# A hand-run list scheduler gets a draft pass, new durations and a table of 262 priority shifts, and tiles are bound to the draft's buffers

## Chip, cores, metric

One core of one Trainium2 chip. The core has five engines with a queue each: TensorE (PE, matrix products), VectorE (DVE), ScalarE (ACT), GpSimd (POOL) and SyncE (SP), which here only issues DMAs. Each engine works through its own queue in order; across engines they synchronise by semaphores. The metric is the device time of one execution in microseconds; lower is better.

## What is computed

A two-layer decoder trunk on 256 tokens of width 2048, all in float32. Each layer is a token mixer and a SwiGLU, each wrapped in an adaLN modulation, a residual and a LayerNorm:

```python
for layer in range(DEPTH):
    shift, scale, gate = _ada(c, ada_w[layer, 0], ada_b[layer, 0])
    h = x * (1.0 + scale) + shift
    y = _mixer_ab(h, ...) if layer % 2 == 0 else _mixer_cd(h, positions, ...)
    x = _layer_norm(ALPHA * x + (1.0 + gate) * y, ln_g[layer, 0], ln_b[layer, 0])
    shift, scale, gate = _ada(c, ada_w[layer, 1], ada_b[layer, 1])
    y = _swiglu(x * (1.0 + scale) + shift, ffn_w_gate[layer], ffn_w_up[layer], ffn_w_down[layer])
    x = _layer_norm(ALPHA * x + (1.0 + gate) * y, ln_g[layer, 1], ln_b[layer, 1])
```

Mixer AB is one input projection, then eight mLSTM heads beside sixteen RWKV-7 heads, then one output projection. Mixer CD is the same with eight retention heads and eight gated-DeltaNet heads. `_ada` is a product of a vector with a 2048 by 6144 matrix. The weights are read once: 677 MB move in one execution.

## The kernel before

**Products.** Every weight is split into a high and a low half (`split`, lines 693 to 715): a 1 MB block is loaded into a `raw` tile by an SP DMA (line 690), ACT copies it to `hi` (line 713), DVE subtracts to get `lo` (line 714). `part` (line 718) then issues three TensorE products for each piece, hi by hi, hi by lo and lo by hi (lines 728 to 730), each with 512 columns in most blocks. One 1 MB block gives 24 such products. They are called the dense products below.

**adaLN.** The vector-matrix products don't use TensorE: `ada_unit` (line 635) loads 1 MB of `ada_w` and DVE multiplies and sums it (line 649). There are 192 such units, 32 of them before the first `h` is whole, the rest spread between the products by `fill`.

**Stages.** In the program's order: `first_products` (the first adaLN units and the first two blocks of columns), `mixer_ab` with `mix_out`, `ffn(0)`, `mixer_cd` with `mix_out`, `ffn(1)`. The mixers hold many small products, transposes and DVE and ACT steps that hang on one another: the triangular inverses (`inverses`, lines 1037 to 1090), the RWKV and mLSTM heads, the DeltaNet chain, and `norm` at the end of each sub-layer. The SwiGLU stages are nearly all dense products.

**Buffers.** Tiles come from pools with tags: `raw` has 3 buffers, `hi` and `lo` 3 each, the 8 KB tag `a` 5, `y` 3, `q4` 4, `tiny` 12; PSUM banks come in three tags (`g` 3, `m` 3, `c` 2). A tile can begin only when a buffer of its tag is free.

**The order.** The kernel doesn't leave the order of each engine's queue to the framework. After the whole program is written out, `Plan` (lines 208 to 526) reads the instruction list, works out the dependencies (`depend`), gives each instruction a duration (`cost`, `matmul`, `prepare`) and runs a list scheduler over a model of the five engines and one DMA pipe (`run`): at each moment an engine takes the ready instruction with the lowest priority number. The model holds a rate for the DMA pipe, a delay between engines, buffers per tag (as a count of free ones, opened in the order of first use), ACT table loads and a TensorE clock that falls to one half after a window of 3413 ns in which TensorE was little used. `impose` (line 522 on) then chains the instructions of each engine in the order found. Only the order is imposed; on the chip each instruction still waits for its semaphores, and which buffer of a tag a tile gets is chosen by the framework. The priorities are those of the program's order with the offsets of `high_priority`. The last lines of `body`:

```python
plan = Plan(tc, tc.nc, 250, k.after)
plan.prepare(0)
order, _ = plan.run([x.bass_priority for x in plan.ins])
plan.impose(order)
```

Of the kernel before, what the change touches and what calls it, by code (L numbers as in the profile page):

```python
# [12 lines left out]
F32 = mybir.dt.float32  # L13
# [190 lines left out]
WINDOW = 3413.0  # L204
SETS = {"Silu": 18, "Tanh": 18, "Sigmoid": 2, "Exp": 0, "Sin": 9}


class Plan:
# [3 lines left out]
    def __init__(self, tc, nc, soon=0.5, after={}):  # L212
        self.tc, self.nc, self.soon, self.rate = tc, nc, soon, 358.0
# [80 lines left out]
    def cost(self, i):  # L294

        x, e = self.ins[i], self.eng[i]
        sizes = []
        for o in list(x.ins) + list(x.outs):
            if hasattr(o, "bass_ap"):
                n = 1  # L300
                for s, c in o.ap[1:]:
                    n *= int(c)
                sizes.append(n)
        n = max(sizes or [1])
        op = x.opcode
        if e == "DVE":
            if op == "TensorScalarPtr":
                if x.is_scalar_tensor_tensor:
                    d = 2373 if len(x.outs) > 1 or n >= 2048 else 150 + n * 1.045 + (55 if n > 100 else 5)
                elif x.is_tensor_tensor_scan:  # L310
                    d = 200 + n * 2.1
                else:
                    ptr = sum(1 for o in list(x.ins)[1:] if hasattr(o, "bass_ap"))
                    d = 145 + n * (0.77 if ptr else 0.55) + (100 if ptr and n > 100 else 0)
            elif op == "TensorCopy":
                ps = any(o.bass_ap.tensor.name in self.psum for o in x.ins if hasattr(o, "bass_ap"))
                d = 150 + n * (1.045 if ps else 0.53)
            else:
                d = {"BNStats": 135 + n * 1.07, "BNStatsAggregate": 168, "StreamShuffle": 179 + n * 1.1, "Memset": 60 + n * 0.5,
                     "Reciprocal": 157 if n < 64 else 150 + 2 * n}.get(op, 150 + n * 1.045)  # L320
            return max(d - 60, 15), d
        if e == "Activation":
            if len(x.outs) > 1:
                d = 500
            else:
                d = 200 + n * 0.83 + (80 if any(hasattr(o, "bass_ap") and k == 1 for o, k in zip(list(x.ins)[1:], sizes[1:])) else 0)
                d = d if n > 64 else max(300, d)
            return max(d - 60, 15), d
        if e == "Pool":
            d = {"TensorScalarAffineSelect": 1130 if n > 300 else 520, "TensorTensor": 1300, "TensorScalarPtr": 1000, "Memset": 100 + n}.get(op, 100)  # L330
            return d, d
        return 50, 50

    def matmul(self, i):

        x = self.ins[i]
        n = int(np.prod([int(c) for s, c in x.outs[0].ap[1:]]))
        w, m = x.ins[0], x.ins[1]
        if "float32r" in str(w.dtype):
            return n / 2.4, 13.5  # L340
        if x.is_transpose:
            return 106.0, 3.0
        k = int(np.prod([int(c) for s, c in m.ap[1:]]))
        return 2 * n / 1.2, 2 * (max(k, n) / 1.2 + 4.5) - 2 * n / 1.2
# [4 lines left out]
    def run(self, priority, clock=True, log=None):  # L349
# [14 lines left out]
        free = {t[0]: t[1] for t in tag.values()}  # L364
# [20 lines left out]
        clk = [1.0, 0, 0.0]  # L385
        for i in range(N):
            if not left[i]:
                heapq.heappush(future[eng[i]], (0.0, priority[i], i))
# [14 lines left out]
        while left_n:  # L403
# [5 lines left out]
            while releases and releases[0][0] <= now:  # L409
                _, t = heapq.heappop(releases)  # L410
                free[t] += 1
                for i in gated.pop(t, ()):
                    heapq.heappush(avail[eng[i]], (priority[i], i))
            again = True
            while again:
                again = False
                for e in E:
# [4 lines left out]
                    while at[e] <= now and a:  # L422
# [6 lines left out]
                        if e == "PE":  # L429
                            st, over = self.pe[i]  # L430
# [14 lines left out]
                        for n in of.get(i, ()):  # L445
                            if n in opened:
                                continue
                            opened.add(n)
                            t = tag[n][0]
                            free[t] -= 1  # L450
                            head[t] += 1
                            for k in gated.pop(t, ()):
                                heapq.heappush(avail[eng[k]], (priority[k], k))
                        start[i] = now
                        if e == "PE":
                            z, rest = now, st
                            while rest > 1e-6:
# [10 lines left out]
                                clk[2] += step  # L468
# [4 lines left out]
                            done[i] = at[e] + 160 / clk[0]  # L473
                        elif i in self.bytes:
                            at[e] = now + 60
                            by = self.bytes[i]
                            dma = max(now + 500, dma) + by / self.rate
                            done[i] = max(dma + 1300, now + 2000)
                        else:
                            x = 0.0  # L480
                            if e == "Activation":
                                s = self.table(i)
                                if s is not None and s != tab:
                                    tab, x = s, 1283.0
                            at[e] = now + x + c
                            done[i] = now + x + d
# [4 lines left out]
                        for n in of.get(i, ()):  # L491
                            remaining[n] -= 1
                            ends[n] = max(ends[n], done[i])
                            if not remaining[n]:
                                heapq.heappush(releases, (ends[n] + 40, tag[n][0]))
                                heapq.heappush(events, (ends[n] + 40, 0))
                        for j in users[i]:
                            left[j] -= 1
                            r = at[e] if e == "PE" and eng[j] == "PE" else done[i] + 40
# [9 lines left out]
    def prepare(self, soon_pe=0.0):  # L509
        self.soon_pe = soon_pe  # L510
        self.costs, self.pe, self.bytes = {}, {}, {}
        for i, x in enumerate(self.ins):
            if self.eng[i] == "PE":
                self.pe[i] = self.matmul(i)
            elif x.opcode == "DMACopy":
                self.costs[i] = 60, 60
            else:
                self.costs[i] = self.cost(i)
# [10 lines left out]
class Trunk:  # L529
    def __init__(self, tc, ins, out, stack):  # L530
        self.tc, self.nc, self.ins, self.out = tc, tc.nc, ins, out
# [21 lines left out]

    def bank(self, kind="m"):

        return {"g": self.ps_g, "c": self.ps_c, "m": self.ps_m}[kind].tile([P, 512], F32, tag=kind, name=self.name(kind))

    def a8(self, shape, dt=F32):
        return self.a_p.tile(shape, dt, tag="a", name=self.name("a"))

    def y8(self, shape):
        return self.y_p.tile(shape, F32, tag="y", name=self.name("y"))

    def q4(self, shape, dt=F32):
        return self.mix.tile(shape, dt, tag="q4", bufs=4, name=self.name("q"))

    def t2(self, shape):
        return self.mix.tile(shape, F32, tag="t2", bufs=3, name=self.name("t"))

    def t1(self, shape):  # L570
        return self.mix.tile(shape, F32, tag="t1", bufs=3, name=self.name("s"))

    def f1(self, shape):
        return self.mix.tile(shape, F32, tag="f1", bufs=3, name=self.name("f"))

    def own(self, shape, tag, bufs, dt=F32):
        return self.mix.tile(shape, dt, tag=tag, bufs=bufs, name=self.name(tag))

    def tiny(self, shape, tag="tiny", bufs=12):
        return self.mix.tile(shape, F32, tag=tag, bufs=bufs, name=self.name("v"))  # L580
# [107 lines left out]
    def raw(self, src, room=None):  # L688
        w = room([P, 2048]) if room else self.raw_p.tile([P, 2048], F32, tag="raw", name=self.name("raw"))
# [3 lines left out]
    def split(self, src, n, ahead=2000, homes="ss", room=None):  # L693
# [3 lines left out]
        with self.tc.high_priority(offset=ahead):  # L697
            w = self.raw(src, room)
            parts = []
            for i, home in enumerate(homes):  # L700
                if home == "s":
                    hi = self.split_p.tile([P, 1024], F32R, tag="hi", name=self.name("hi"))
                    lo = self.split_p.tile([P, 1024], F32R, tag="lo", name=self.name("lo"))
# [188 lines left out]
    def norm(self, y, banks, stats, sub):  # L892
# [3 lines left out]
        acts = [self.h_p.tile([P, 2, 4, T], F32R, tag="h", name=self.name("h")) for _ in range(KG)]  # L896
# [435 lines left out]
    def first_products(self):  # L1332
# [7 lines left out]
        for g in range(KG):  # L1340
            h.append(self.h_p.tile([P, 2, 4, T], F32R, tag="h", name=self.name("h")))
# [553 lines left out]
def body(tc, ins, out):  # L1895
    with ExitStack() as stack:
        k = Trunk(tc, ins, out, stack)
# [18 lines left out]
OUT = "y_out"  # L1916

# [14 lines left out]
```

## Time and profile before

| | us |
|---|---|
| median of 3 runs | 2728.81 |
| fastest, slowest of the 3 | 2728.55, 2734.14 |
| the profiled execution's own time | 2744.2 |
| its span, first to last instruction | 2742.5 |
| TensorE busy in it | 2631.8 (96%) |
| VectorE busy in it | 2002.3 (73%) |
| ScalarE busy in it | 1272.7 (46%) |
| mean granted TensorE clock | 0.977 |

A busy share says that an engine had an instruction in work; for TensorE the end of an instruction is modelled, so a string of products with short stalls between them still shows as busy. The granted clock is the share of full speed that the throttle gave TensorE. The span is cut below into the kernel's stages: start (0 to 137 us), mixer AB with its output projection (137 to 754), first SwiGLU (754 to 1439), mixer CD (1439 to 2056), second SwiGLU (2056 to 2673), and the end.

### The profile page before, as it was taken

To read this page: it belongs to the slowest core of one execution; us is meant where nothing else is said; L and a number is where in the kernel's file an instruction comes from. 1 tells how busy PE (TensorE), PEld (TensorE's weight loads), DVE (VectorE), ACT (ScalarE), POOL (GpSimd) and SP (SyncE) were. 2 spreads that over 40 slices of the span, in tenths; PEclk is the share of its full clock that TensorE was granted. 3 is DMA by queue.
4 is the path that set the end of the run, shared out by engine and by line. 5 is a ranking of instruction groups with operands and counts; after the bars stand their busy time and mean duration, and the time that the engine had idled before them with its cause. 6 is when DMAs were issued, how large, how long until landed. Compare 5 with 4: busy or idle time off the path is not lost.

```text
span 2742.5 us, 33594 instructions
## 1 busy us (share of the span) xinstructions
PE 2631.8 (96%) x12906; PEld 2164.2 (79%) x12906; DVE 2002.3 (73%) x3153; ACT 1272.7 (46%) x1706; POOL 72.3 (3%) x88
## 2 busy tenths in 40 slices
PE   5699999999999999999999999999999999999997
PEld 3578777778788888888888888878878888888886
DVE  7897868878777777767777989776866665557457
ACT  2364445556644444434446554444454444443442
POOL 0000000110000000000000101000000000000000
PEclk8799989999999999999999999999999999999999
DMA  9967647555588788868856775675657675556554
GB/s 394 370 244 259 226 176 282 183 187 190 205 311 309 305 323 311 315 234 302 309 201 223 270 274 224 234 259 200 244 200 275 249 289 203 196 200 227 187 186 167
DMA packets 105659, 681.60 MB, mean 249 GB/s; under 512 B 11861, under 2 KB 15129, under 8 KB 27417
## 3 DMA queue, kind: packets, MB, share of 16 engines
q1 hardware_dynamic: 104346, 677.36, 66.7%
q8 instruction: 101, 1.65, 0.2%
q10 hardware_dynamic: 1152, 2.10, 0.2%
q14 instruction: 60, 0.49, 0.1%
HBM read 668.89 MB, written 10.52 MB: 248 GB/s over the span
## 4 chain that ended last, share of the span: by engine, by line
PE 78%; DVE 10%; DMA 8%; ACT 2%; issue 2%; SPq 0%; POOL 0%; DVEq 0%; ACTq 0%
PE g L728 24%; PE g L729 23%; PE g L730 23%; DVE lo L714 2%; DMA raw<-ada 2%; DMA a<-ada 2%; DVE raw L649 2%; DMA raw<-w_ab 1%; ACT hi L713 1%; DMA za<-ada 1%; PE m L973 1%; DMA y<-w_ab 1%; PE m L1253 0%; PE m L1086 0%; PE m L1271 0%
## 5 line engine op out<-in xcount | busy, mean ns | idle before, releaser
L714 DVE TENSOR_TENSOR lo<-raw,hi 128x1024 fp32r<-128x1024 f32 (+2 forms) x802 | 971.5, 1214 | 580.6 <-ACT hi L713 577.1
L713 ACT ACTIVATE hi<-raw 128x1024 fp32r<-128x1024 f32 (+2 forms) x802 | 842.6, 1052 | 1111.4 <-PE g L730 1035.5
L728 PE MATMUL g<-hi,h 128*128 128x512 f32 (+2 forms) x2312 | 911.0, 394 | 41.2 <-ACT h L792 37.3
L729 PE MATMUL g<-lo,h 128*128 128x512 f32 (+2 forms) x2312 | 908.3, 393 | 2.1 <-DVE lo L714 2.1
L730 PE MATMUL g<-hi,h 128*128 128x512 f32 (+2 forms) x2312 | 907.1, 393 | 0.0
L728 PEld LDWEIGHTS g<-hi,h 128*128 128x128 f32 x2312 | 440.6, 191 | 132.8 <-ACT h L792 40.1
L729 PEld LDWEIGHTS g<-lo,h 128*128 128x128 f32 x2312 | 440.5, 191 | 92.5 <-issue 4.3
L730 PEld LDWEIGHTS g<-hi,h 128*128 128x128 f32 x2312 | 440.1, 190 | 88.2 <-issue 3.6
L729 PE MATMUL g<-lo,a 128*128 128x512 f32 x920 | 359.0, 390 | 1.6 <-DVE lo L714 1.6
L728 PE MATMUL g<-hi,a 128*128 128x512 f32 x920 | 359.3, 391 | 0.0
L730 PE MATMUL g<-hi,a 128*128 128x512 f32 x920 | 358.8, 390 | 0.0
L649 DVE SCALAR_TENSOR_TENSOR raw<-raw,silu_c 128x2048 f32<-128x2048 f32 x82 | 187.4, 2286 | 32.1 <-DMA raw<-ada 24.3
L729 PEld LDWEIGHTS g<-lo,a 128*128 128x128 f32 x920 | 172.8, 188 | 37.0 <-DVE lo L714 2.0
L730 PEld LDWEIGHTS g<-hi,a 128*128 128x128 f32 x920 | 172.8, 188 | 35.6
L728 PEld LDWEIGHTS g<-hi,a 128*128 128x128 f32 x920 | 172.7, 188 | 35.5
L649 DVE SCALAR_TENSOR_TENSOR za<-za,silu_c 128x2048 f32<-128x2048 f32 x56 | 127.9, 2284 | 4.5 <-DMA za<-ada 4.5
L649 DVE SCALAR_TENSOR_TENSOR zt<-zt,silu_c 128x2048 f32<-128x2048 f32 x38 | 86.8, 2285 | 2.6 <-DMA zt<-ada 2.4
L1437 DVE SCALAR_TENSOR_TENSOR f<-c,cols_sb,f 128x253 f32<-128x253 f32 (+2 forms) x120 | 55.8, 476 | 4.4 <-ACT f L1434 3.9
L1638 POOL TENSOR_SCALAR s<-cons_sb,log_alpha 128x128 f32<-128x128 f32 x16 | 13.4, 852 | 1008.5 <-DVE log_alpha L1582 871.6
L649 DVE SCALAR_TENSOR_TENSOR a<-a,silu_c 128x2048 f32<-128x2048 f32 x16 | 36.3, 2285 | 0.0
L911 ACT ACTIVATE t<-m,affine 128x128 f32<-128x128 f32 x96 | 34.9, 469 | 0.1
L1094 POOL TENSOR_SCALAR_AFFINE_SELECT a<-a 128x512 f32<-128x512 f32 (+1 forms) x20 | 22.4, 1127 | 332.4 <-ACT a L1255 300.0
(480 smaller groups left out, 2122.2 us busy)
## 6 DMA issues: line engine op xcount, KB each, us to landing
raw<-gu SPq DMA_DIRECT2D x176, 1024.0 KB, 4.8
raw<-dn SPq DMA_DIRECT2D x88, 1024.0 KB, 4.8
raw<-ada SPq DMA_DIRECT2D x82, 1024.0 KB, 6.1
raw<-w_cd SPq DMA_DIRECT2D x60, 1024.0 KB, 4.8
za<-ada SPq DMA_DIRECT2D x56, 1024.0 KB, 7.0
raw<-w_ab SPq DMA_DIRECT2D x48, 1024.0 KB, 4.9
zt<-ada SPq DMA_DIRECT2D x38, 1024.0 KB, 7.1
a<-ada SPq DMA_DIRECT2D x16, 1024.0 KB, 17.1
```

The source lines that it names most:

```text
L649: v.scalar_tensor_tensor(w[:], w[:], 1.0, self.sc[:], ALU.mult, ALU.mult, accum_out=m[:, i:i + 1])
L713: nc.scalar.activation(hi[:, :2 * n], ws, AF.Copy)
L714: nc.vector.tensor_tensor(lo[:, :2 * n], ws, hi[:, :2 * n], ALU.subtract)
L728: mm(o, ah, wh, start=start and k == 0, stop=False)
L729: mm(o, ah, wl, start=False, stop=False)
L730: mm(o, al, wh, start=False, stop=stop and k == 3)
L911: nc.scalar.activation(h32[:, j, :], b[:, P * j:P * j + P], AF.Identity, bias=self.ab[:, sub + 1, 16 + k:17 + k], scale=self.ab[:, sub + 1 ...
L973: nc.tensor.transpose(b[:, P * k:P * k + P], gs[:, t, P * k:P * k + P], self.ident)
L1094: self.nc.gpsimd.affine_select(x, x, pattern=[[0, n] for n in dims] + [[1, P]], compare_op=ALU.is_gt if strict else ALU.is_ge, fill=0.0, b ...
L1437: v.scalar_tensor_tensor(o[:, d:T], b[:, T * j:T * j + T - d], self.col(wname, 4 * (tile0 + i + j) + 3 - d), o[:, d:T], ALU.mult, ALU.add)
L1638: nc.gpsimd.tensor_scalar(L[:], sl, self.gl[:, t, 4 * g + j:4 * g + j + 1], None, ALU.mult)
```

## The change

No instruction of the computation is added or removed. What changes is the order within each engine's queue and the buffer each tile uses.

1. **Two builds.** `kernel` builds the program twice. The first build runs `Plan.run` and raises `Drafted` with the order of each engine and the buffer that the model gave each tile. The second build writes the same program out again and imposes that order.
2. **Buffers.** In the second build each tile that goes through the new `Trunk.get` asks for a tag of its own buffer (`a.3`, say) with one buffer, the one that the draft gave it. The model now keeps a list of free buffers of each tag instead of a count and takes the one that was freed first.
3. **Durations.** `cost`, `matmul` and `prepare` get new constants, among them factors by engine (`MARGINS`), a DMA rate of 396 instead of 358, a DMA landing time and a delay between engines of 67 instead of 40 ns. The clock model counts small products at a part of their time, and a change of the shape of the products costs 92 ns.
4. **Priorities.** A table `PLACES` of 262 pairs adds a shift to the priority of each instruction from the given index on, up to the next pair.

```diff
+MARGINS = {'Activation': 0.9875423830141832, 'DVE': 1.0101153058187327, 'PE': 1.014122181386299, 'Pool': 1.1973257770806474}
+LAND, CROSS, RATE, SOON = 2471.8499431610267, 67.12701229691764, 396.01772112428813, 250.0
+PLACES = (
+    (0, 240), (16, 0), (18, 920), (21, 0), (31, 920), (32, 40), (58, 0), (212, -1920), (216, 0), (225, -1680), (277, -1920), (281, 0), (303, -1000),
+    (325, -8960), (340, -9280), (347, -8120), (373, 120), (380, -1080), (397, -7480), (406, 0), (476, -80), (531, -840), (560, 0), (568, -200),
...
+    (15285, 48.0463), (16983, 160), (17012, 0), (17182, -1720), (17198, 0), (17201, -360), (17208, -420),
+)
...
-                    d = 2373 if len(x.outs) > 1 or n >= 2048 else 150 + n * 1.045 + (55 if n > 100 else 5)
+                    d = 2285 if len(x.outs) > 1 or n >= 2048 else 150 + n * 1.045 + (55 if ptr and n > 30 else 0)
...
-            return max(d - 60, 15), d
+            return max(d - 82, 15), d
         if e == "Activation":
-            if len(x.outs) > 1:
-                d = 500
-            else:
-                d = 200 + n * 0.83 + (80 if any(hasattr(o, "bass_ap") and k == 1 for o, k in zip(list(x.ins)[1:], sizes[1:])) else 0)
-                d = d if n > 64 else max(300, d)
-            return max(d - 60, 15), d
+            d = 310 if len(x.outs) > 1 else 163 + n * 0.848 + (0 if ps else 35) + (0, 97, 190)[ptr]
+            return max(d - 100, 15), d
...
-        return 2 * n / 1.2, 2 * (max(k, n) / 1.2 + 4.5) - 2 * n / 1.2
+        r = int(m.ap[0][1])
+        if max(r, k, n) <= 32:
+            return 30.0, 10.0, 1
+        return 2 * n / 1.2, 2 * (max(k, n) / 1.2 + 4.8) - 2 * n / 1.2, (0 if r > 64 else 2 if r > 32 else 3)
...
-        free = {t[0]: t[1] for t in tag.values()}
+        free = {t[0]: list(range(t[1])) for t in tag.values()}
+        self.held = held = {}
...
-                            free[t] -= 1
+                            held[n] = free[t].pop(0)
...
+                            if form != shape:
+                                shape, over = form, over + 92
...
-                                clk[2] += step
+                                clk[2] += step * (1.0, 0.25, 0.5, 0.25)[form]
...
-                            dma = max(now + 500, dma) + by / self.rate
-                            done[i] = max(dma + 1300, now + 2000)
+                            dma = max(now + self.iss, dma) + by / self.rate
+                            done[i] = dma + self.land
...
+    def get(self, pool, shape, dt, tag, bufs, name):
+
+        name = self.name(name)
+        if name in self.slots:
+            tag, bufs = f"{tag}.{self.slots[name]}", 1
+        return pool.tile(shape, dt, tag=tag, bufs=bufs, name=name)
+
...
-        plan = Plan(tc, tc.nc, 250, k.after)
-        plan.prepare(0)
-        order, _ = plan.run([x.bass_priority for x in plan.ins])
+        plan = Plan(tc, tc.nc, SOON, k.after)
+        if draft is None:
+            plan.prepare(0)
+            shift = np.zeros(len(plan.ins))
+            for i, s in PLACES:
+                shift[i:] = s
+            order, _ = plan.run([x.bass_priority + s for x, s in zip(plan.ins, shift)])
+            raise Drafted(order, {n.rsplit("_", 1)[0]: s for n, s in plan.held.items()})
         plan.impose(order)
```

More of the change, by code (lines that the diff above doesn't have):

```diff
@@ L212, in __init__ @@
     def __init__(self, tc, nc, soon=0.5, after={}):
-        self.tc, self.nc, self.soon, self.rate = tc, nc, soon, 358.0
+        self.tc, self.nc, self.soon, self.rate = tc, nc, soon, RATE
         self.ins = [x for x in nc.cur_bb.bb.instructions if x.opcode != "TilePoolBoundary"]
@@ L296, in cost @@
         x, e = self.ins[i], self.eng[i]
[L297 to L304, printed above, removed]
+        size = lambda o: int(np.prod([int(c) for s, c in o.ap[1:]]))
+        aps = [o for o in x.ins if hasattr(o, "bass_ap")]
+        outs = [o for o in x.outs if hasattr(o, "bass_ap")]
+        n = max([size(o) for o in aps + outs] or [1])
+        ptr = sum(1 for o in aps[1:] if size(o) == 1)
+        ps = any(o.bass_ap.tensor.name in self.psum for o in aps + outs)
         op = x.opcode
@@ L312, in cost @@
                 else:
-                    ptr = sum(1 for o in list(x.ins)[1:] if hasattr(o, "bass_ap"))
                     d = 145 + n * (0.77 if ptr else 0.55) + (100 if ptr and n > 100 else 0)
             elif op == "TensorCopy":
-                ps = any(o.bass_ap.tensor.name in self.psum for o in x.ins if hasattr(o, "bass_ap"))
                 d = 150 + n * (1.045 if ps else 0.53)
             else:
-                d = {"BNStats": 135 + n * 1.07, "BNStatsAggregate": 168, "StreamShuffle": 179 + n * 1.1, "Memset": 60 + n * 0.5,
-                     "Reciprocal": 157 if n < 64 else 150 + 2 * n}.get(op, 150 + n * 1.045)
-            return max(d - 60, 15), d
+                d = {"BNStats": 135 + n * 1.07, "BNStatsAggregate": 175, "StreamShuffle": 175 + n * 1.05, "Memset": 100 + n * 0.5,
+                     "Reciprocal": 150 + n * 6}.get(op, 150 + n * 1.045)
+            return max(d - 82, 15), d
         if e == "Activation":
-            if len(x.outs) > 1:
-                d = 500
-            else:
-                d = 200 + n * 0.83 + (80 if any(hasattr(o, "bass_ap") and k == 1 for o, k in zip(list(x.ins)[1:], sizes[1:])) else 0)
-                d = d if n > 64 else max(300, d)
-            return max(d - 60, 15), d
+            d = 310 if len(x.outs) > 1 else 163 + n * 0.848 + (0 if ps else 35) + (0, 97, 190)[ptr]
+            return max(d - 100, 15), d
         if e == "Pool":
-            d = {"TensorScalarAffineSelect": 1130 if n > 300 else 520, "TensorTensor": 1300, "TensorScalarPtr": 1000, "Memset": 100 + n}.get(op, 100)
+            d = {"TensorScalarAffineSelect": 1100 if n == 512 else 900, "TensorTensor": 950, "TensorScalarPtr": 1200, "Memset": 610}.get(op, 100)
             return d, d
@@ L385, in run @@
         clk = [1.0, 0, 0.0]
+        shape = 0
         for i in range(N):
@@ L409, in run @@
             while releases and releases[0][0] <= now:
-                _, t = heapq.heappop(releases)
-                free[t] += 1
+                _, t, n = heapq.heappop(releases)
+                free[t].append(held[n])
                 for i in gated.pop(t, ()):
@@ L429, in run @@
                         if e == "PE":
-                            st, over = self.pe[i]
+                            st, over, form = self.pe[i]
                             hold = self.soon_pe
@@ L472, in run @@
                             at[e] = z + over / clk[0]
-                            done[i] = at[e] + 160 / clk[0]
+                            done[i] = at[e] + self.pel / clk[0]
                         elif i in self.bytes:
@@ L498, in run @@
                             left[j] -= 1
-                            r = at[e] if e == "PE" and eng[j] == "PE" else done[i] + 40
+                            r = at[e] if e == "PE" and eng[j] == "PE" else done[i] + self.lat
                             if r > ready[j]:
@@ L510, in prepare @@
         self.soon_pe = soon_pe
+        self.iss, self.land, self.pel, self.lat = 1300.0, LAND, 160.0, CROSS
         self.costs, self.pe, self.bytes = {}, {}, {}
@@ L513, in prepare @@
             if self.eng[i] == "PE":
-                self.pe[i] = self.matmul(i)
+                st, over, form = self.matmul(i)
+                self.pe[i] = st * MARGINS["PE"], over, form
             elif x.opcode == "DMACopy":
@@ L517, in prepare @@
             else:
-                self.costs[i] = self.cost(i)
+                self.costs[i] = tuple(c * MARGINS[self.eng[i]] for c in self.cost(i)) if self.eng[i] in MARGINS else self.cost(i)
             if x.opcode == "DMACopy":
@@ L529, with __init__ @@
 class Trunk:
-    def __init__(self, tc, ins, out, stack):
-        self.tc, self.nc, self.ins, self.out = tc, tc.nc, ins, out
+    def __init__(self, tc, ins, out, stack, slots):
+        self.tc, self.nc, self.ins, self.out, self.slots = tc, tc.nc, ins, out, slots
         def pool(name, bufs, **kw):
@@ L688, in raw @@
     def raw(self, src, room=None):
-        w = room([P, 2048]) if room else self.raw_p.tile([P, 2048], F32, tag="raw", name=self.name("raw"))
+        w = room([P, 2048]) if room else self.get(self.raw_p, [P, 2048], F32, "raw", 3, "raw")
         self.load = self.nc.sync.dma_start(w[:, :src.shape[-1]], src).ins.name
@@ L701, in split @@
                 if home == "s":
-                    hi = self.split_p.tile([P, 1024], F32R, tag="hi", name=self.name("hi"))
-                    lo = self.split_p.tile([P, 1024], F32R, tag="lo", name=self.name("lo"))
+                    hi = self.get(self.split_p, [P, 1024], F32R, "hi", 3, "hi")
+                    lo = self.get(self.split_p, [P, 1024], F32R, "lo", 3, "lo")
                 elif home == "a":
@@ L895, in norm @@
         self.ada(max(0, 48 * sub + 80 - self.ada_next))
-        acts = [self.h_p.tile([P, 2, 4, T], F32R, tag="h", name=self.name("h")) for _ in range(KG)]
+        acts = [self.get(self.h_p, [P, 2, 4, T], F32R, "h", 4, "h") for _ in range(KG)]
         dst = self.dram.tile([T, D], F32, name=self.name("x"))
@@ L1340, in first_products @@
         for g in range(KG):
-            h.append(self.h_p.tile([P, 2, 4, T], F32R, tag="h", name=self.name("h")))
+            h.append(self.get(self.h_p, [P, 2, 4, T], F32R, "h", 4, "h"))
             xs = [self.first_x(g, i) for i in range(2)]
@@ L1892, in mix_out, with body @@
         return self.norm(y, banks, stats, sub)
-def body(tc, ins, out):
+class Drafted(Exception):
+    pass
+def body(tc, ins, out, draft=None):
+    order, slots = draft or (None, {})
     with ExitStack() as stack:
-        k = Trunk(tc, ins, out, stack)
+        k = Trunk(tc, ins, out, stack, slots)
         k.setup()
@@ L1909, in body, with build @@
         k.ffn(1, x, h)
-        plan = Plan(tc, tc.nc, 250, k.after)
-        plan.prepare(0)
-        order, _ = plan.run([x.bass_priority for x in plan.ins])
+        plan = Plan(tc, tc.nc, SOON, k.after)
[6 more added lines that the diff above has]
+            raise Drafted(order, {n.rsplit("_", 1)[0]: s for n, s in plan.held.items()})
         plan.impose(order)
 OUT = "y_out"
+def build(bacc, tile, arrays, draft):
+    nc = bacc.Bacc("TRN2", target_bir_lowering=False, num_devices=1, dynamic_dma_scratch_size=1024)
+    ins = {k: nc.dram_tensor(k, a.shape, mybir.dt.from_np(a.dtype), kind="ExternalInput").ap() for k, a in arrays.items()}
+    out = nc.dram_tensor(OUT, (T, D), F32, kind="ExternalOutput").ap()
+    with tile.TileContext(nc) as tc:
+        body(tc, ins, out, draft)
+    return nc
 def kernel(**inputs):
@@ L1924 @@
     arrays = lay_out(**{k: np.asarray(v) for k, v in inputs.items()})
-    nc = bacc.Bacc("TRN2", target_bir_lowering=False, num_devices=1, dynamic_dma_scratch_size=1024)
-    ins = {k: nc.dram_tensor(k, a.shape, mybir.dt.from_np(a.dtype), kind="ExternalInput").ap() for k, a in arrays.items()}
-    out = nc.dram_tensor(OUT, (T, D), F32, kind="ExternalOutput").ap()
-    with tile.TileContext(nc) as tc:
-        body(tc, ins, out)
+    try:
+        build(bacc, tile, arrays, None)
+    except Drafted as d:
+        draft = d.args
+    nc = build(bacc, tile, arrays, draft)
     r = run_bass_kernel_spmd(nc, [arrays], core_ids=[0])
```

24 lines of the change are left out of this document (12 added, 12 removed), and 22 rows, old and new, of the table PLACES.

## The prediction

> **What bounds the kernel now.** I read the page's busy times and its slices first, then a table of busy time by stage, then who waits for whom.
>
> ```profile
> PE 2631.8 (96%) x12906; PEld 2164.2 (79%) x12906; DVE 2002.3 (73%) x3153; ACT 1272.7 (46%) x1706; POOL 72.3 (3%) x88
> ...
> PEclk8799989999999999999999999999999999999999
> ...
> GB/s 394 370 244 259 226 176 282 183 187 190 205 311 309 305 323 311 315 234 302 309 201 223 270 274 224 234 259 200 244 200 275 249 289 203 196 200 227 187 186 167
> ...
> 0.00:137.00 137.00, 78.39 (x291) 61.15 (x292) 110.66 (x126) 45.14 (x63) 0.28 (x5) 0.81 0.95 382
> 137.00:754.00 617.00, 593.57 (x3364) 478.21 (x3363) 495.12 (x1145) 334.06 (x575) 35.71 (x47) 0.96 0.60 217
> 754.00:1439.00 685.00, 685.00 (x3065) 567.14 (x3064) 499.16 (x496) 293.48 (x302) 0.00 (x0) 1.00 0.77 292
> 1439.00:2056.00 617.00, 604.04 (x3194) 503.05 (x3194) 493.93 (x969) 318.38 (x479) 36.30 (x36) 0.99 0.64 236
> 2056.00:2673.00 617.00, 616.83 (x2760) 510.39 (x2759) 352.92 (x334) 263.35 (x273) 0.00 (x0) 1.00 0.62 224
> 2673.00:2742.00 69.00, 53.92 (x238) 44.28 (x236) 50.53 (x84) 18.25 (x18) 0.00 (x0) 0.91 0.45 168
> ```
>
> A stage row gives the stretch and its length, busy time with count of PE, PEld, DVE, ACT and POOL, then the granted clock, the DMA share and GB/s. TensorE is the bound, but not everywhere alike. In the two SwiGLU stages (685 and 617 us) it works without a break at full clock: in 1302 us no order can gain. What an order can reach lies elsewhere:
>
> - start: 137.0 - 78.4 = 58.6 us idle, beside a DMA share of 0.95;
> - mixer AB: 617.0 - 593.6 = 23.4 us idle, and 4% of the clock, 617 x 0.04 = 24.7 us;
> - mixer CD: 617.0 - 604.0 = 13.0 us idle, and 617 x 0.01 = 6.2 us;
> - end: 69.0 - 53.9 = 15.1 us.
>
> Since a busy PE can hide short stalls, I check AB by counting. Below are the first and the last of 28 dense products in a row from the timeline (start, length), the row of the tiles `g`, which nearly all dense products write, for AB, and a run of 16 small products from the chain.
>
> ```profile
> 799.81 0.39 PE L729 MATMUL g<-lo,h 128*128 128x512 f32 x1
> ...
> 805.93 0.39 PE L729 MATMUL g<-lo,h 128*128 128x512 f32 x1
> ...
> 137.00:754.00 617.00, 430.28 (x1693) 316.09 (x1694) 5.22 (x8) 20.00 (x34) 0.96 0.60 217
> ...
> 451.75 1.79 PE m L1037 x16
> ```
>
> 27 steps in 805.93 - 799.81 = 6.12 us are 0.227 us for one dense product; 1693 of them are 384 us. A small one takes 1.79 / 16 = 0.112 us; the other 3364 - 1693 = 1671 are then about 187 us. 617 - 384 - 187 = 46 us are left, against 23.4 + 24.7 = 48 us that idle time and clock show. The estimate is rough (wider forms cost more, packed ones less), but it finds the same loss, so I work with the visible one.
>
> Whom TensorE waits for in AB, then in CD, then in the start (waiter, releaser: us in total, times, longest):
>
> ```profile
> PE c L1201 <- DVE za L1104: 4.6, 2, 2.5
> PE m L908 <- ACT y L903: 1.9, 2, 1.4
> ...
> PE m L908 <- ACT y L903: 4.1, 4, 1.7
> PE m L1079 <- DVE a L1071: 1.7, 2, 1.5
> ...
> PE g L728 <- ACT h L792: 46.7, 7, 13.0
> ```
>
> In the mixers there is no single large wait, only many of one or two microseconds, each where an instruction at the head of TensorE's queue waits for a DVE or ACT step while dense products that could run stand behind it. That is what an order can mend.
>
> **The change, part by part.** *Instructions.* None is added or removed, so every engine's work stays; all that can change is who stands where.
>
> *Durations.* I compare the model's new constants with the trace.
>
> ```profile
> 113.17 2.28 DVE L649 SCALAR_TENSOR_TENSOR raw<-raw,silu_c 128x2048 f32<-128x2048 f32 x1
> 115.38 0.08 DVE L649 DVE_READ_ACCUMULATOR raw<-raw,silu_c 128x1 f32 x1
> 115.38 1.22 DVE L714 TENSOR_TENSOR zt<-y,zt 128x1024 fp32r<-128x1024 f32 x1
> ...
> L911 ACT ACTIVATE t<-m,affine 128x128 f32<-128x128 f32 x96 | 34.9, 469 | 0.1
> L903 ACT ACTIVATE y<-y,v,v 128x512 f32<-128x512 f32 x24 | 18.3, 811 | 10.8 <-DVE v L922 10.8
> ...
> raw<-gu SPq DMA_DIRECT2D x176, 1024.0 KB, 4.8
> ```
>
> An adaLN unit holds DVE for 115.38 - 113.17 = 2.21 us. The old model says 2373 - 60 = 2313 ns, the new one (2285 - 82) x 1.0101 = 2225 ns: the old one had 0.10 us too much in each of 192 units. For the ACT step of line 911 the old model gives 200 + 128 x 0.83 + 80 = 386 ns, the new one (163 + 128 x 0.848 + 190) x 0.9875 = 456 ns, against 469 measured; for line 903 it is 705 and 822 x 0.9875 = 812, against 811. So on DVE and ACT the draft lies much nearer to the chip, and just in the chains that TensorE waits for. Two constants lie further off: a dense product is 213.3 x 1.0141 + 13.5 = 229.8 ns against 227 (old: 226.8), and a 1 MB load takes 1.3 + 1048576 / 396000 + 2.47 = 6.4 us against a median of 4.8. Both are on the careful side: they ask for loads early, and cost nothing while a buffer is free.
>
> *Clock.* The old model counts a small product as full activity. In the new one, 32-row and 64-row products count a quarter or a half, so that a stretch full of them (the inverses) shows as one in which the clock falls. CD holds inverses, too, and keeps 0.99 where AB keeps 0.96; I take CD as the mark for what an order reaches. AB then regains 24.7 - 6.2 = 18.5 us. The bounds are 0 and 24.7.
>
> *Idle time.* By the same mark AB falls from 23.4 to 13.0 us, a gain of 10.4; bounds 0 and 23.4. For CD there is no mark inside this trace. I take a third of its 13.0 + 6.2 = 19.2 us, 6 us, since the waits on line 903 there are at the layer's end, behind a LayerNorm that needs the last products; bounds 0 and 19.2.
>
> *Start.* DMA limits it, so products moved forward must find their weights loaded. The first slice moves 394 GB/s, the stage 382 (stage row above). At the best rate throughout, 137 x (1 - 382 / 394) = 4 us go. The large shifts early in the table (-8960 at index 325) move work forward here; bounds 0 and, were the whole of the waits on line 792 filled, 46.7, which a DMA share of 0.95 excludes; I take 4.
>
> *End.* DVE works alone behind the last product; each step needs the one before. Three table entries change its neighbours; I take 0, bounds -1 and 1.
>
> *SwiGLU stages.* 0, since neither has idle time. Cover: one 1 MB block feeds TensorE for 24 x 0.227 = 5.4 us, so three `raw` buffers hold 16 us against a load of 4.8. Were a load held up by more than 11 us, it would show.
>
> *Buffers.* Each tile is bound to the buffer that the draft gave it; formerly the framework chose by its own view of time. Nothing is issued for it. It adds no wait if tiles come free in the draft's order. If two come free the other way round, the next tile waits for the later one, and behind it on SP's queue stand all later loads, whose `hi` and `lo` TensorE needs. SP waits for buffers already:
>
> ```profile
> SPq L690 <- DVE lo L714: 1520.5, 322, 16.1
> SPq L690 <- DVE raw L649: 169.4, 34, 9.2
> ```
>
> So the mean such wait is 1520.5 / 322 = 4.7 us, and it is harmless where the next load has cover. Below nothing the price can go too: where the framework had chosen an unlucky buffer, binding takes the wait away. The trace shows no wait by buffer number, so I can bound this only: one `lo` step (115.38 to the next start, 1.14 us, nearly its 1.22) more or less at each of the stalls in the mixers. 36.4 us of idle time in pieces of some 1 us are 36 stalls, so -41 to +41 us. I take 0, since dense stages have cover.
>
> Sum: 18.5 + 10.4 + 6 + 4 = 38.9, say 38 us less. The profiled span of 2742.5 becomes 2704.5, and the execution, 2744.2 with what lies around the span, 2706. That execution took 15.4 us more than the median; the same 38 us off 2728.8 give **2691 us**.
>
> **What a page of the Trainium skill says against it.** TensorE: Matmul & The Clock Gate (Part 1) says that the clock is gated by a window of about 3.4 us which runs freely and doesn't begin with the kernel, so that its phase differs from run to run, and advises not to fit to it. By that rule an order fitted to window edges would not keep the 18.5 us, and the sum would be 38 - 18.5, or 2709. The trace leans against it: three runs of one order lie within 2728.55 to 2734.14, so phase alone moves this kernel by 5.6 us at most.
>
> **Rivals.**
>
> 1. *The clock stays.* The order removes waits, but AB's clock stays at 0.96. Then 38 - 18.5 = 19.5 us: 2709. For it: AB has more small products (1671 of 3364) than any stage. Against: CD's 0.99.
> 2. *The search found nearly all.* 262 shifts on a model that is close for DVE and ACT fill the mixers: 48.1 + 19.2 + 4 = 71 us, 2658. Against: the waits behind LayerNorm and inverses are real chains.
> 3. *Nothing changes.* The stalls move to other places, since DVE is 495 of 617 us busy in AB and sets the pace of every chain: 2729.
> 4. *Slower: the order is too tight.* TensorE, DVE and SP run in order. The draft sets an instruction just after the moment at which its model has the operand and buffer ready; where the chip is later, everything behind stands. Place: the mixers, where DVE is 80% busy. Price: half of the bound above, one `lo` step at every other of 36 stalls, 20 us, with no gain: 2749. It decides once real lateness exceeds the work queued between producer and consumer, about one dense group of 3 products, 0.7 us.
>
> **How the numbers follow.** Forecast (2675 to 2700): 0.40. Clock stays: 0.20. Nearly all: 0.12. Nothing: 0.12. Slower: 0.16. This kernel's measurement can tell 0.2%, 5.5 us, from no change. Faster is 0.40 + 0.20 + 0.12 = 0.72, same 0.12, slower 0.16. The range reaches from a little under the second rival, 2655, to 2736, which takes in no change and the forecast with the upper bound of the buffers (2691 + 41 = 2732): left out are a part of "nearly all" and most of "slower", about 2 in 10.
>
> **What would show it.** Right: instruction counts as before; the SwiGLU stretches at full PE and as long; the mixer AB with a granted clock of 0.98 or more and under 15 us idle; span near 2704. The clock rival: AB at 0.96 with less idle time. The slower one: new waits of PE on `lo`, or of SP on single buffers, of over 1 us in the mixers. Wrong altogether: a SwiGLU stage with idle time, which would mean that loads lost their cover.

## The result, and the profile after

The changed kernel takes 2700.3 us (median of 4 runs, 2695.0 to 2710.2) against 2730.1 beside it: a ratio of 0.9891, 95% interval 0.9869 to 0.9913. Timed once more among the experiments it took 2701.9 us (6 runs), a ratio of 0.9902 (0.9876 to 0.9928). That is 30 us less in the first set and 26 in the second; the forecast was 38 less, 2691 us, within a range of 2655 to 2736.

The page of the changed kernel, with the rows that stand in the prediction for the kernel before; the code has moved down by 37 lines, so that the dense products are now lines 765 to 767:

```profile
PE 2616.7 (97%) x12906; PEld 2157.6 (80%) x12906; DVE 2003.0 (74%) x3153; ACT 1270.1 (47%) x1705; POOL 87.1 (3%) x88
...
PEclk9899998999999999999999999999999999999999
```

The busy times by stretch (PE, PEld, DVE, ACT, POOL with counts, then clock, DMA share, GB/s), with the same limits as before:

```profile
0.00:137.00 137.00, 78.62 (x312) 61.40 (x313) 113.24 (x134) 48.78 (x69) 0.29 (x5) 0.89 0.97 388
137.00:754.00 617.00, 606.75 (x3436) 493.30 (x3436) 505.33 (x1151) 338.47 (x577) 41.48 (x47) 0.97 0.62 225
754.00:1439.00 685.00, 683.88 (x3067) 565.73 (x3066) 503.87 (x538) 300.95 (x322) 0.00 (x0) 1.00 0.78 290
1439.00:2056.00 617.00, 609.66 (x3239) 508.84 (x3238) 497.84 (x931) 313.69 (x463) 45.29 (x36) 1.00 0.68 245
2056.00:2673.00 617.00, 617.00 (x2768) 511.59 (x2767) 355.50 (x343) 263.03 (x273) 0.00 (x0) 1.00 0.62 219
2673.00:2708.00 35.00, 20.77 (x92) 16.76 (x90) 27.18 (x59) 5.20 (x5) 0.00 (x0) 0.86 0.39 147
```

The same 12906 instructions on TensorE, in less time; ACT has one table load less (1705 instructions for 1706). TensorE's idle time fell in the mixers: in AB from 23.4 to 617.0 - 606.8 = 10.2 us, in CD from 13.0 to 7.3. In the start it is 58.4 us, as before (58.6). The clock rose in the start (0.81 to 0.89), in AB (0.96 to 0.97) and in CD (0.99 to 1.00).

Since the stages end at other times now, I date them by the first transpose of each of the three inner LayerNorms, in the timelines of the kernel before (line 908) and after (line 945):

```profile
710.79 0.44 PE L908 MATMUL m<-cons_sb,y 128*128 128x128 f32 x2 [0.49 <-ACT y L903]
...
1445.86 0.33 PE L908 MATMUL m<-cons_sb,y 128*128 128x128 f32 x1 [0.53 <-ACT y L903]
...
1989.83 0.44 PE L908 MATMUL m<-cons_sb,y 128*128 128x128 f32 x2 [0.50 <-ACT y L903]
```

```profile
691.35 0.44 PE L945 MATMUL m<-cons_sb,y 128*128 128x128 f32 x2 [0.49 <-ACT y L940]
...
1425.17 0.42 PE L945 MATMUL m<-cons_sb,y 128*128 128x128 f32 x2
...
1957.18 0.44 PE L945 MATMUL m<-cons_sb,y 128*128 128x128 f32 x2 [0.62 <-ACT y L940]
```

From the start to the first norm 19.4 us are gone; from the first to the second (SwiGLU) 735.1 became 733.8; from the second to the third (CD) 544.0 became 532.0; from there to the end 752.7 became 751.3. In this pair of executions start and AB together give more than half, CD a third, the SwiGLU stages nearly nothing. The pair isn't typical: the execution of before took 2744.2 us. A second trace of the same order, in `old_model_bound` below (2724.0 us), has its first norm at 698.7 us and takes 536.2 us through CD; against that one start and AB give 7.3 us and CD 4.2.

Many small waits of TensorE went. In AB (137 to 740 us) of the changed kernel the largest left are

```profile
PE m L1290 <- DVE a L1293: 2.8, 7, 0.8
PE c L1238 <- DVE e L1057: 1.5, 1, 1.5
```

The wait on the shifted channels (`PE c L1201 <- DVE za L1104`, 4.6 us before) isn't among those listed; the same line of TensorE, now 1238, waits 1.5 us for another step.

### The profile page after: what moved, and what is told of

It reads as the page before. It is cut to its first block, busy times and chain, and to the rows that moved or that the text cites. A ratio compares the mean times of both kernels' runs of the same rounds, so it can differ in the third digit from the quotient of the medians.

```text
span 2708.5 us, 33578 instructions
## 1 busy us (share of the span) xinstructions
PE 2616.7 (97%) x12906; PEld 2157.6 (80%) x12906; DVE 2003.0 (74%) x3153; ACT 1270.1 (47%) x1705; POOL 87.1 (3%) x88
## 4 chain that ended last, share of the span: by engine, by line
PE 86%; DVE 7%; DMA 4%; ACT 1%; issue 1%; POOL 0%; SPq 0%; DVEq 0%; ACTq 0%
PE g L765 26%; PE g L766 26%; PE g L767 26%; DMA raw<-ada 2%; DVE lo L751 1%; DMA a<-ada 1%; DMA y<-w_ab 1%; PE m L1010 1%; DVE raw L686 1%; ACT hi L750 1%; PE m L1290 0%; PE m L1312 0%; PE c L1468 0%; PE m L1308 0%; PE m L1321 0%
## 5 line engine op out<-in xcount | busy, mean ns | idle before, releaser
L1675 POOL TENSOR_SCALAR s<-cons_sb,log_alpha 128x128 f32<-128x128 f32 x16 | 28.7, 1806 | 997.0 <-DVE log_alpha L1619 853.9
L765 PE MATMUL m<-hi,h 128*128 128x512 f32 x24 | 11.2, 468 | 23.6 <-ACT h L829 23.6
```

The source lines that it names most:

```text
L765: mm(o, ah, wh, start=start and k == 0, stop=False)
L1675: nc.gpsimd.tensor_scalar(L[:], sl, self.gl[:, t, 4 * g + j:4 * g + j + 1], None, ALU.mult)
```

## The experiments

Three causes were in question: the nearer durations, the searched table, and the binding of buffers. Beside them stood the question how much of a clock gain lasts from run to run. Each kernel was timed in several rounds beside the kernel before (medians of 2726.6 to 2728.9 us in the three sets). Kernels of different sets are compared by their ratios to the kernel before; 0.001 of a ratio is 2.7 us.

**The parts by themselves.** First the changed kernel with an empty table (`no_shifts`):

```diff
-            for i, s in PLACES:
+            for i, s in ():
```

> The changed kernel with an empty table of shifts: new durations, new clock model and binding stay. If the nearer durations carry the gain, 2700 to 2710 us. If the searched shifts carry it, 2725 or more (2730 is the kernel before). Between, both have a part. Mixer stages are read by the times at which the LayerNorm transposes of the three inner norms begin (711, 1446, 1990 us before; 691, 1425, 1957 after).

Measured: 2737.7 us (12 runs), ratio 1.0029 (1.0013 to 1.0045). Not only is the gain gone, the kernel is 8 to 9 us slower than the one before. The durations that lie nearer to the trace give nothing by themselves.

The table alone, on the old `cost`, `matmul`, rate, landing and delay (`old_model_shifts`; the lines shown stand for the whole model):

```diff
-            return max(d - 82, 15), d
+            return max(d - 60, 15), d
...
-                                shape, over = form, over + 92
+                                shape, over = form, over
```

> The table of shifts on the old durations and the old clock model, with binding. If the shifts say something about the kernel that holds whatever the model, 2700 to 2715 us. If they are fitted to the new model and are noise without it, 2725 to 2760.

Measured: 2745.5 us (7 runs), ratio 1.0067 (1.0041 to 1.0093). On another model the table does harm.

Then the binding. `no_binding` has the draft's order and leaves the buffers to the framework:

```diff
-            raise Drafted(order, {n.rsplit("_", 1)[0]: s for n, s in plan.held.items()})
+            raise Drafted(order, {})
```

> The changed kernel with the draft's order, row for row, but with the framework choosing the buffers. If binding costs and gives nothing, 2700 us within 5. If the framework's choice is unlucky and binding takes waits away, 2710 to 2730. If binding holds up loads, 2690 or less.

Measured: 2694.4 us (6 runs), ratio 0.9884 (0.9858 to 0.9911); repeated,

> The changed kernel's order with the framework's buffers, once more. If binding does nothing, its times overlap with those of the changed kernel and the medians lie within 5 us; if binding costs, it stays 6 us faster.

it took 2708.5 us (6 runs, 2690.6 to 2714.3), ratio 0.9909 (0.9883 to 0.9934). The changed kernel's ten runs, 2691.2 to 2718.8, lie in the same span. The first six runs looked 6 us faster than the changed kernel and the second six 6.6 us slower; the means over all are 2701.9 us (10 runs) with binding and 2700.3 (12 runs) without. The order of before with bound buffers, `old_model_bound`, which is `old_model_shifts` with the empty table:

> The order of the kernel before, row for row, with each tile bound to the buffer of the old model's draft. If binding costs and gives nothing, 2730 us within 5. If it is a part of the gain by itself, 2710 to 2724. If it holds up loads, 2736 or more.

Measured: 2725.4 us (12 runs), ratio 0.9995 (0.9978 to 1.0012). No effect of binding shows under either order; with this spread one of up to some 7 us would not be seen under the changed order, of some 5 us under the order of before.

**The table by stages.** Each of these kernels keeps the shifts of one range of indices and sets the others to zero:

```diff
-                shift[i:] = s
+                shift[i:] = s if 488 <= i < 4738 else 0
```

> The changed kernel with the shifts of the first 488 instructions alone (the start stage), all later ones zero. If each stage's shifts work in their own stage, the loss up to the first 100 us of TensorE work falls by about 6 us, as between the kernel without shifts and the changed one, and the time is 2732 us, against 2738 without shifts. If an earlier start also carries the clock into the mixer, 2725 or less.

Measured: 2717.9 us (12 runs), ratio 0.9967 (0.9953 to 0.9982). By the ratios that is 17 us less than without shifts, where 6 were expected of the start stage.

> The shifts of mixer AB and its output projection alone (indices 488 to 4737). Up to the first inner norm the changed kernel is 24 us (in one profile) to 40 us (in another) ahead of the one without shifts, about 6 of it in the start; so 2704 to 2720 us if the gain is made here. If the gain needs the start or later stages together, 2725 or more.

Measured: 2714.0 us (6 runs), ratio 0.9957 (0.9940 to 0.9974), by the ratios 20 us less than without shifts.

> The shifts of mixer CD alone (indices 9107 to 13038). From the first norm behind the first SwiGLU to the norm behind the mixer the kernel without shifts takes 535.4 us, the changed one 532.0: so 2734 us, hardly to be told from 2738. If CD were as large a part as its idle time before suggested (a third of 19 us and more), 2731 or less.

Measured: 2732.2 us (12 runs), ratio 1.0025 (1.0005 to 1.0044), by the ratios 1 us less, which the intervals can't tell from nothing. The three together are 38 us, and the whole table gives 35 to 38 (0.9902 and 0.9891 against 1.0029): within the noise the ranges add up. The 39 shifts of the remaining ranges were not timed alone. But the start's shifts are worth more than their own stage, since they also act in AB. The stretches of start and AB, first without shifts, then with those of the start:

```profile
0.00:137.00 137.00, 79.04 (x289) 62.23 (x290) 110.28 (x133) 45.35 (x62) 0.29 (x5) 0.84 0.94 378
137.00:754.00 617.00, 593.74 (x3346) 475.98 (x3345) 493.70 (x1136) 333.78 (x574) 35.91 (x47) 0.96 0.60 216
```

```profile
0.00:137.00 137.00, 77.49 (x310) 60.35 (x311) 113.03 (x132) 48.16 (x69) 0.28 (x5) 0.89 0.96 387
137.00:754.00 617.00, 600.35 (x3423) 483.80 (x3422) 504.89 (x1151) 342.17 (x579) 39.44 (x47) 0.98 0.62 223
```

In the start TensorE is as idle as before (59.5 against 58.0 us), yet 310 products are done instead of 289, at a clock of 0.89 instead of 0.84. Its waits on `h` have been gathered into fewer, longer ones, which may be why the clock is higher; that was not tried. The waits of the changed kernel's start show the gathering (7 waits with a longest of 13.0 us in the kernel before):

```profile
PE g L765 <- ACT h L829: 28.0, 4, 12.7
PE m L765 <- ACT h L829: 23.6, 1, 23.6
```

In the 617 us of AB, where no priority was moved, TensorE works off another 77 products and is idle for 16.7 us instead of 23.3: what the start delivers earlier, and in another order, reshuffles the stage behind it.

**How firm is the table?** One constant of the model moved by 1% (`rate_392`):

```diff
-LAND, CROSS, RATE, SOON = 2471.8499431610267, 67.12701229691764, 396.01772112428813, 250.0
+LAND, CROSS, RATE, SOON = 2471.8499431610267, 67.12701229691764, 392.0, 250.0
```

> The changed kernel with one constant of the model moved by 1%: a DMA rate of 392 instead of 396. If the table of shifts says something of the kernel, 2700 us within 5. If it is fitted to one course of the draft and falls to pieces with it, 2712 or more.

Measured: 2725.3 us (12 runs), ratio 0.9983 (0.9969 to 0.9998). 25 of the 30 us are gone. The runs fall into two groups, five of 2713.9 to 2717.2 us with a clock of 0.987 or 0.988 and seven of 2724.9 to 2728.3 with 0.983 or 0.984. The profiled execution is of the second group, and there the loss lies in AB:

```profile
137.00:754.00 617.00, 597.80 (x3353) 480.75 (x3353) 495.57 (x1139) 330.40 (x568) 38.41 (x47) 0.96 0.60 216
```

19.2 us idle and a clock of 0.96 again. The start's row is unchanged at 312 products and 0.89. And the same 1% without any shifts (`no_shifts_392`):

> No shifts, new durations, binding, and the model's DMA rate 392 instead of 396. If the 2738 us of the kernel without shifts says something of the new durations, 2738 within 4. If an unsearched draft is a draw that any small change of a constant makes anew, more than 5 us away, somewhere in 2715 to 2745.

Measured: 2725.3 us (12 runs), ratio 0.9991 (0.9979 to 1.0002), by the ratios 10 us less than at 396. So the 2738 of the kernel without shifts says little of its durations: an unsearched draft is like a draw, and one small change made a new one. The drafts here lie at 2725 to 2729 (old durations), 2738 and 2725 (new ones), and with a table that doesn't fit at 2746 and 2725. At 392 the table and the empty table differ by 0.0008 of the ratio, less than the intervals.

**More of the same.** A table searched further on the kernel's own model, for the mean of four phases of the clock window (`more_search`, 286 shifts in place of 262):

> The changed kernel with a table searched further (286 shifts) for the mean of four phases of the clock window instead of one. If fitting to one phase costs the changed kernel, 2690 us or less and a narrower spread; if the table is already at its end, 2700 us within 5.

Measured: 2700.9 us (5 runs, 2693.1 to 2708.9), ratio 0.9890 (0.9874 to 0.9906). The further search found nothing that the chip shows, and no version here is clearly faster than the changed kernel.

**The clock.** Each run comes with the mean clock that TensorE was granted. The changed kernel beside the last set:

> The changed kernel itself, once more, beside the others on one chip. If the run-to-run spread of one order is the phase of the clock, its times spread over some 15 us and follow the mean granted clock at some 2.4 us for 0.001, as those of the kernel before do; 2695 to 2710 us, median 2700.

Measured: 2701.9 us (6 runs, 2691.2 to 2718.8). 2691.2 us had a clock of 0.991, 2718.8 had 0.982: (2718.8 - 2691.2) / 9 = 3.1 us for 0.001. Over all runs, a straight line through the 70 of the kernel before (2716.3 us at 0.986 to 2741.3 at 0.977) gives 2.2 us for 0.001, and through the 22 with the changed order (10 of the changed kernel, 12 with unbound buffers) 2.5. One order of instructions thus spreads over 25 us and more, where some 15 were expected. The clock accounts for 96% of the variance in the changed order and for 75% in the kernel before. It isn't so in every order: the six runs of `shifts_ab` lie within 3.5 us at clocks of 0.983 to 0.987.

The traces show how. The changed kernel and `no_binding` have the same order; here are stretches of both at the same times, first the changed kernel's:

```profile
420.00:430.00 10.00, 9.57 (x153) 7.69 (x152) 9.30 (x22) 5.92 (x13) 0.00 (x0) 1.00 0.79 286
430.00:440.00 10.00, 9.89 (x53) 8.76 (x53) 4.81 (x8) 5.36 (x10) 0.00 (x0) 0.58 0.54 204
440.00:450.00 10.00, 10.00 (x46) 9.40 (x47) 2.35 (x4) 3.39 (x9) 0.00 (x0) 0.56 0.35 131
```

```profile
430.00:440.00 10.00, 10.00 (x71) 8.55 (x69) 6.32 (x16) 4.34 (x11) 0.00 (x0) 1.00 0.43 136
440.00:450.00 10.00, 8.78 (x43) 5.76 (x42) 8.30 (x34) 5.41 (x18) 2.25 (x2) 1.00 0.61 210
```

In the one execution the clock fell to one half for 17 us, in the other it didn't; the two spans are 2708.5 and 2692.4 us. What stood on TensorE at the fall, and at the return, from the changed kernel's timeline and its stretches of 2 us:

```profile
428.23 1.14 PE L1116 MATMUL m<-y,a 64*64 64x64 f32 x16 [0.21 <-DVE y L1108]
...
430.11 1.14 PE L1123 MATMUL m<-y,P 64*64 64x64 f32 x16 [0.32 <-ACT P L1120]
...
438.28 0.63 PE L1320 MATMUL m<-q,a 128*128 128x64 f32 x2
...
443.79 0.77 PE L766 MATMUL g<-lo,h 128*128 128x512 f32 x1
...
446.07 0.63 PE L765 MATMUL g<-hi,h 128*128 128x512 f32 x1
```

```profile
430.00:432.00 2.00, 1.89 (x22) 1.82 (x22) 1.35 (x1) 1.08 (x4) 0.00 (x0) 0.91 0.98 415
432.00:434.00 2.00, 2.00 (x11) 2.00 (x11) 0.95 (x2) 1.61 (x2) 0.00 (x0) 0.50 0.34 87
...
446.00:448.00 2.00, 2.00 (x10) 1.83 (x9) 0.00 (x0) 0.44 (x2) 0.00 (x0) 0.50 0.56 217
448.00:450.00 2.00, 2.00 (x15) 1.99 (x15) 0.05 (x1) 0.29 (x1) 0.00 (x0) 0.82 0.00 0
```

Two runs of 16 small products of the inverses come before the fall. Then TensorE is busy without a gap, mostly with products of 64 columns, and the clock stays at one half; it returns some 2 us after a group of six dense products, the longest dense run of the stretch. Busy time alone did not bring it back.

The lengths show a grid. The fourteen traces hold 120 stretches at half clock that end inside the span, and each is a whole multiple of 3.413 us long, from one to ten; the one above is five, 17.07 us, from 431.64 to 448.71. So the clock changes at the edges of a grid of that step, and where the grid lies against the work differs between executions. Below are the grid steps with the small products, first the changed kernel's, in which both runs of 16 (428.23 and 430.11) lie and after which the clock falls, then that of `no_binding`, where an edge stands at 422.43, between the starts of its two runs (421.31 and 423.19):

```profile
428.23:431.64 3.41, 3.08 (x38) 2.76 (x39) 2.12 (x6) 2.75 (x8) 0.00 (x0) 1.00 1.01 419
```

```profile
422.43:425.84 3.41, 3.08 (x33) 2.88 (x33) 2.29 (x3) 2.35 (x7) 0.00 (x0) 1.00 0.89 371
```

TensorE is as busy in the one as in the other, and neither holds a dense product; only the first is followed by half clock. In the second traces of the two kernels it is the same: both runs in one step and a fall (`after_again`), an edge close to the start of the second run and none (`no_binding_again`). So in four of four traces this fall goes with the place of the grid. What the clock counts stays open: in `more_search`, another order, a step with little more than the second run (428.09 to 431.50) was followed by a fall too.

## Why the prediction was right, and where not

**Sum and direction: right.** 30 us less instead of 38, in the stages named, with the SwiGLU stages as long as before to within 1.4 us each. The forecast case (2675 to 2700) ends at 2700, so the result stands on its upper edge. Of the signs that were named, the idle time in AB came out (10.2 us, under 15), the clock there didn't (0.97 in the profiled execution, where 0.98 or more was asked and 0.96 would have spoken for the clock rival).

**Idle time: right in size, rather too large.** Forecast were 10.4 us in AB, 6 in CD and 4 in the start, 20 together. The two profiles show 23.4 - 10.2 = 13.2 in AB, 13.0 - 7.3 = 5.7 in CD and 0.2 in the start, 19 together. Against the second trace of the order of before (18.7 us idle in AB, 9.7 in CD, 60.2 in the start) it is 8.5, 2.4 and 1.8, or 13.

**Clock: right in kind, too large.** The term was 18.5 us, from AB's 0.96. The mean clock of the kernel before is 0.9827 over 70 runs, that of the changed order 0.9879 over 22; 0.0052 at 2.2 to 2.5 us for 0.001 is 11 to 13 us. Of the difference of the means, 2728.0 - 2701.0 = 27 us, the other 14 to 16 don't go with the clock and are put down to stalls; the 13 to 19 us of idle time above agree. The term was mis-sized in the main because the profiled execution (2744.2 us at 0.977) was an unlucky one, slower than any of the 70. The order of before, traced again in `old_model_bound`, has in AB

```profile
137.00:754.00 617.00, 598.33 (x3426) 482.53 (x3425) 503.30 (x1153) 339.61 (x581) 35.85 (x47) 0.98 0.62 223
```

a clock of 0.98, not 0.96, and 18.7 us idle. I had noted that this execution took 15.4 us more than the median, and took the same 38 us off both; its surplus was largely the clock loss that I then counted as a gain. Nor was the gain where the term put it. In the two profiles the time at half clock went from 51.2 to 30.7 us in the start, from 17.1 to 3.4 in CD, and in AB only from 44.4 to 41.0; at most half of each is lost, so up to 10.2, 6.8 and 1.7 us were gained. AB's clock differs between executions of the changed order: 0.97 in both traces with bound buffers, 1.00 in both with unbound ones, whose grids lie otherwise; over all runs the mean clocks are 0.9877 and 0.9880.

**The free window: dismissed on too few runs.** I held three runs within 5.6 us against a phase that differs from run to run, "at most" as I wrote. The profiled execution, 2744.2 us and of the same order, was already there and lay 10 us above the slowest of the three. Seventy runs of one order span 25 us. The Trainium skill, TensorE: Matmul & The Clock Gate (Part 1), says that the window runs freely, so that the phase differs between runs. The spread and the grid above agree. The rival that I drew from it, no clock gain at all, did not come true: 11 to 13 us went with the clock in the mean, since the changed order spends less time at half clock, not none (4 to 9 stretches that end inside the span in its four traces, against 12 and 11 in the two of the order of before). The clock rival's 2709 is outside the interval of the ratio (0.9869 to 0.9913 of 2730.1, 2694 to 2706).

**Durations: the argument that failed.** The prediction argued that the draft "lies much nearer to the chip", and rested the gain on that; the table had no part of its own in the sum but for the start. Without the table the nearer durations gave 2738 and, at a DMA rate of 392, 2725, no better than the old ones' 2725. What carries the gain is the searched table: it picks one draft out of many, and on the two other models on which it was timed it did not work (2746 on the old one, 2725 after 1%). The nearer durations may matter for the search, since a course picked on a false model need not be fast on the chip; a search on the old model was not tried, so that stays open.

**Start: right in size by another route, and its effect went further.** I took 4 us there, from a higher DMA rate. The rate rose from 382 to 388 GB/s, which by the same sum is 137 x (1 - 382 / 388) = 2 us, and the idle time didn't change. But 312 products were done in the stage instead of 291, at a clock of 0.89 instead of 0.81; at 0.227 us each, were all of them dense, that is 4.8 us. The start's shifts alone are worth 17 us, most of it in AB: in the traces the first norm comes at 694.6 us with them and at 715.7 us without any.

**Buffers: right.** 0 was taken, with 41 either way; two pairs show nothing beyond their spread. SP still waits on `lo` as it did (1520.5 us in 322 waits before):

```profile
SPq L727 <- DVE lo L751: 1501.0, 326, 10.4
```

**The slower rival** (order too tight) didn't decide for this table; but `old_model_shifts` shows that an order can be 0.7% slower with the same instructions, and 2746 is near the 2749 that was priced. That nearness is luck, since the mechanism was not the one named: its trace has less idle time in AB (14.9 us) than that of `old_model_bound` (18.7) and no wait there above 2.7 us in total. It has more time at half clock (102.4 us against 75.1, the last stretch, which runs past the end, left out), of which at most half, 13.7 us, is lost, and 3.6 us more idle time in the start; its span is 21.5 us longer.

## What to carry to other kernels

An imposed order worked out on a model should be judged by several draws: change a constant by 1% and see how far the time moves before giving a constant credit. A table of searched priorities can be bound to the exact model it was searched on: both changes of the model that were tried here took its gain away, so after such a change it has to be timed, and if need be searched, anew. Where the clock gate of TensorE is in play, read the granted clock of several runs before a profiled execution's clock loss enters a sum.

## What the runs showed of the hardware

The granted clock was either one or one half, and all 120 stretches at half clock that end inside a span are whole multiples of 3.413 us long. One of them lasted 17.07 us under a TensorE that the profile shows fully busy, and ended after a group of six 512-column products; products of 64 columns did not bring the clock back. In another execution of the same order the same products ran at full clock, so they don't by themselves bring it down; it fell where both runs of 16 products of 64 by 64 lay in one step of the grid. On POOL the 16 steps of line 1675 (line 1638 before, 852 ns each) took more than twice as long in the changed order, though the kernel as a whole is faster:

```profile
L1675 POOL TENSOR_SCALAR s<-cons_sb,log_alpha 128x128 f32<-128x128 f32 x16 | 28.7, 1806 | 997.0 <-DVE log_alpha L1619 853.9
```

It goes with the order: 1805 or 1806 ns in all four traces of the changed order, 852 and 964 in the two of the order of before. What slows them was not tried.
